# Low parts of dense weights computed on VectorE alone, and weighted expert scores made two experts ahead, in a two-block transformer kernel

## The chip, the cores and the metric

The kernel runs on one core of one Trainium2 chip, as one launch. The metric is the device time of that launch in microseconds (us). A chip core has TensorE (PE; its weight loads are listed apart as PEld), VectorE (DVE), ScalarE (ACT), GpSimd (POOL) and SyncE (SP), each with its own in-order queue, and DMA queues that move data between memory and the on-chip SBUF.

## The reference

Two blocks, in float32, on 256 tokens of width 1024.

The first block has two layers. Each layer is half a SwiGLU feed-forward (width 2816), a mixer, and half a second feed-forward:

```python
x = x + 0.5 * swiglu(rmsnorm(x, norm_g[i, 0]), ffn_w_up[i, 0], ffn_w_down[i, 0])
h = rmsnorm(x, norm_g[i, 1])
mix = pool_layer(...) if kind == 0 else diff_layer(...)   # DEPTH = 2: layer 0 pools, layer 1 attends
x = x + mix
x = x + 0.5 * swiglu(rmsnorm(x, norm_g[i, 2]), ffn_w_up[i, 1], ffn_w_down[i, 1])
```

The pooling layer takes windowed means, the differential layer subtracts two softmaxes per head, and both have four heads that attend to a memory of 256 tokens. The second block modulates its norms by six vectors made from `silu(c) @ w_ada`, runs a mixer of block attention and top-k attention (8 heads each, width 64), and ends in a layer of 16384 experts:

```python
q = (hc @ w_query).reshape(B, T_CHUNK, PEER_HEADS, 2, PEER_DKEY // 2)
s = jnp.einsum('bthpd,hpnd->bthpn', q, sub_keys)          # top 16 of 128 twice, then top 16 of 256 sums
g = jax.nn.softmax(g_s, axis=-1)
act = jax.nn.gelu(jnp.einsum('btd,bthkd->bthk', hc, u_emb[e_idx]), approximate=False)
return jnp.einsum('bthk,bthkd->btd', g * act, v_emb[e_idx])
```

## The kernel before

The kernel keeps all activations on chip and streams some 790 chunks of weights, each 128 x 1024 floats (512 KB), through four or five raw buffers. Every chunk is used in a three-product form. ScalarE rounds the raw chunk to a high part `whi` (line 144), a second engine computes the low part `wlo = raw - whi` (line 145), and TensorE adds three products: high by high, high by low, low by high (`mm3`, lines 184 to 186). The activations are split into high and low parts in the same way (`split_evac`, lines 194 and 195).

The order of work is the order in which the Python code emits instructions: the schedule is manual, and each engine runs its own instructions strictly in that order. The list `items` holds the chunks in order of use. `nextw` (line 153) hands the next chunk to TensorE's code, and before that emits the splits of the chunks up to `cfg["ahead"]` beyond it; `split_one` (line 130) emits one split: the load of a chunk further on, `whi` on ScalarE, `wlo` on VectorE or GpSimd. Which of the two is set in line 134 by `cfg["pool"]`: with 3, every third chunk goes to GpSimd; with 1, all of them; with 0, none. The feed-forward stages and projections run with 3, the attention stages (pooling layer's memory heads, differential attention, second block's attention, and the query projection of the experts) with 1 or 2, and the expert stages with 0.

In a feed-forward (`ffn`, line 499) each block of 512 up-columns makes a gate: VectorE multiplies the products by the row scale (line 524), ScalarE applies Silu, GpSimd multiplies by the row scale again (line 526), and VectorE multiplies by the second half of the products (line 536). Between the blocks VectorE also accumulates `silu(c) @ w_ada` (`ada_piece`, line 459, with the accumulation in line 469).

The attention stages are software pipelines (`pipeline`, line 50) of units: scores on TensorE, maximum and scale on VectorE (`nb`, line 865 in differential attention), exponential on ScalarE, normalization on VectorE (lines 878 and 880 there, 577 in memory heads, 1164 in the second block), transposition on TensorE. Weight projections are stepped between the units.

In the expert layer each block of 128 experts is called an expert here; there are NE = 128 of them. For each, a u chunk gives activations (`s_step`, line 1320: 24 matmuls of 256 columns, then Gelu on ScalarE in line 1331), and a v chunk gives outputs (12 matmuls of 512 columns for one expert). 78 of the u chunks are done before the first v chunk. After that the v chunks are mixed with the remaining 50 u chunks, one u after every two or three v. Before an expert's v products, `w_step` (line 1495) multiplies its activations by its routing weights: `wf` on VectorE (line 1497), `wh` on ScalarE (line 194), `wl` on VectorE (line 195). `w_step(n + 1)` is emitted at the start of expert n, right behind the split of a chunk two items on; the tiles `wf`, `wh`, `wl` have two buffers each. In this text the v stage is the stretch from the first v product (1624 us) to the end, and an item is one u or v chunk of it.

Of the kernel before, what the change touches and what calls it, by code (L numbers as in the profile page):

```python
# [9 lines left out]
F32 = mybir.dt.float32  # L10
F32R = mybir.dt.float32r
# [4 lines left out]
OP = mybir.AluOpType  # L16
# [3 lines left out]
P = 128  # L20
D = 1024
S = 256
# [7 lines left out]
NE = 128  # L30
# [29 lines left out]
def kernel(ctx: ExitStack, tc: tile.TileContext, A, LAY, stop=None):  # L60
    nc = tc.nc
    ctx.enter_context(tc.manual_schedule())
    V, ACT, G, PE = nc.vector, nc.scalar, nc.gpsimd, nc.tensor
# [39 lines left out]
    deferred = []  # L103
    cfg = {"raw": 5, "ahead": 4, "pool": 3, "phase": 0}
    CH = 1024
# [24 lines left out]
    def split_one():  # L130
        j = st["split"]
        load_to(j + cfg["raw"])
        _, nk, w, call = items[j][:4]
        eng = G if cfg["pool"] and (j + cfg["phase"]) % cfg["pool"] == 0 else V
        n = nk * w
        r = st["raw"].pop(j)
        if call is not None:
            call(r[:, :n].rearrange("p (k w) -> p k w", w=w))
        else:
            p_ = wpool2 if j < dense and st["nsplit"] % 2 else wpool  # L140
            st["nsplit"] += 1
            hi = p_.tile([P, CH], F32R, name="whi", tag="whi", bufs=4)
            lo = p_.tile([P, CH], F32R, name="wlo", tag="wlo", bufs=4)
            ACT.activation(hi[:, :n], r[:, :n], AF.Copy)  # L144
            eng.tensor_tensor(lo[:, :n], r[:, :n], hi[:, :n].bitcast(F32), op=OP.subtract)  # L145
            st["s"][j] = Split(hi[:, :n].rearrange("p (k w) -> p k w", w=w), lo[:, :n].rearrange("p (k w) -> p k w", w=w))
        st["split"] += 1
        load_to(j + 1 + cfg["raw"])
# [245 lines left out]
    def out_proj_k(segs, update, nxt, tail=2, ahead=None):  # L394


        p = [[pmm() for _ in range(2)] for _ in range(NT)]
        n = len(segs)

        def mm(t, h, gis, gots):  # L400
            for gi in gis:
                act, k0 = segs[gi]
                for c, k, _ in gots[gi][h]:
                    mm3(p[t][h], act[:, k0 + k, t * P:(t + 1) * P], c[:, k, :], gi == 0 and k == 0, gi == n - 1 and k == 1)

        gots = {}
        for gi in range(n - tail):
            gots[gi] = [fetch(1), fetch(1)]
            for t in range(NT):
                for h in range(2):  # L410
                    mm(t, h, [gi], gots)
                if t:
                    run_deferred()
                yield
        was = dict(cfg)
        cfg.update(ahead=8 - 2 * tail)
        if tail == 2 and nxt.deep:
            cfg["pool"] = 2
        for gi in range(n - tail, n):
            gots[gi] = [fetch(1), fetch(1)]  # L420
        cfg.update(was)
        for t in range(NT):
            for h in range(2):
                cut = n - 1 if nxt.deep and t and h else n
                mm(t, h, range(n - tail, cut), gots)
                if cut < n:
                    was = dict(cfg)
                    cfg.update(ahead=0, pool=1)
                    ahead.append(fetch(4))
                    nxt.realT(0)  # L430
                    mm(t, h, range(cut, n), gots)
                    if tail > 2:
                        split_more(1)
                update(t, h, p[t][h])
                nxt.pre(t, h)
                if not nxt.deep and (t or h):
                    nxt.T(*((0, 0), (0, 1), (1, 0))[2 * t + h - 1])
                if h:
                    nxt.stats(t)
                if cut < n:  # L440
                    if tail == 2:
                        cfg.update(pool=2, phase=1)
                    ahead.append(fetch(4))
                    cfg.update(was)
                yield
        if not nxt.deep:
            nxt.late = [lambda: nxt.T(1, 1)]
# [48 lines left out]
    def ffn(n, nxt, stk):  # L496
# [17 lines left out]
        for t, p in enumerate(proj_row(hT, 4, n.before)):  # L514
            r = n.rstd[:, t:t + 1]
            ACT.activation(s0[:, t], p[:, :256], AF.Silu, scale=r)
            V.scalar_tensor_tensor(g0[:, t], p[:, 256:], r, s0[:, t], op0=OP.mult, op1=OP.mult)
        rbb = bcast_rows(rb, n.rstd)
        for b in range(1, 11):
            s = fp.tile([P, 2, S], F32, name="silu", tag="silu", bufs=2)  # L520

            def evac(c0, m, p):
                if c0 == 0:
                    V.tensor_tensor(s, p, rbb, op=OP.mult)
                    ACT.activation(s, s, AF.Silu)
                    G.tensor_tensor(s, s, rbb, op=OP.mult)
                    flush()
# [161 lines left out]
    lo = [mem_T(0, 0), mem_T(0, 1)]  # L689
    cfg["pool"] = 0  # L690
    split_one()
# [3 lines left out]
    for f in lo:  # L695
        f()
    cfg.update(pool=3, phase=1, ahead=0)
    p = [pmm() for _ in range(NT)]
# [18 lines left out]
    for l in range(2):  # L717
# [8 lines left out]
        for i, _ in enumerate(proj_cols(mT, 4, 4, lambda c0, m, p, l=l: V.tensor_tensor(KT[l][:, c0:c0 + m, :], p, rbb, op=OP.mult))):  # L726
            if l == 0:
                n0.T(i // 2, i % 2)
    cfg["phase"] = 0
    sng = small([P, 1], "sng", bufs=1)  # L730
# [28 lines left out]
    with pool("pl") as sp:  # L759
# [45 lines left out]
        drain(u_part(0), proj_cols(hT, 4, 4, lambda c0, m, p: ACT.activation(qT[:, c0:c0 + m, :], p, AF.Copy)))  # L805
        cfg["pool"] = 1
        o = out_proj_k([(cat, k) for k in range(0, 12, 2)], plain_add, n2)
        fill = itertools.chain(u_part(1), mixed(), o)
        counts = [0, 1, 1, 0, 1, 1, 1, 2] + [1] * 6
        for n, _ in zip(counts, pipeline(units, [(1, 2), (3, 3), (None, 0), (0, 0), (2, 2)])):  # L810
            for _ in range(n):
                step(fill)
        cfg["pool"] = 3
        drain(fill)
# [15 lines left out]
    with pool("df") as sp:  # L830
# [119 lines left out]
        drain(qk(k[0]), qk(q[0]))  # L950
        cfg["pool"] = 1
        units = [make(t, h) for g in range(2) for t in range(NT) for h in (4 * g, 4 * g + 2)]
# [5 lines left out]
        for i, _ in enumerate(pipeline(units, [(5, 6), (1, 2), (4, 4), (None, 0), (6, 6), (0, 0), (3, 3), (2, 2)])):  # L958
            for _ in range(counts[i] if i < len(counts) else 1):
                step(fill)  # L960
        cfg["pool"] = 3
        drain(o)
# [106 lines left out]
    ACT.activation(iqT, iqp.rearrange("p (j t) -> p j t", j=2), AF.Copy)  # L1069
    cfg.update(pool=3, phase=1)  # L1070
    split_more(4)
    cfg.update(pool=3, phase=0)
    ACT.activation(av[:, 1, :512], mvp[1], AF.Copy)
# [127 lines left out]
    drain(*se)  # L1201
    cfg["pool"] = 1
    nhh = iter(("aq", "ak"))
# [84 lines left out]
    keep_rows(0, 1, q_rows(0, 1))  # L1288
    cfg["pool"] = 2
    split_more(4)  # L1290
# [3 lines left out]
    pop()  # L1294
    cfg["pool"] = 1
    late_scores = []
# [19 lines left out]
    dp = ctx.enter_context(pool("dq", side="right"))  # L1316
    cfg.update(raw=4, ahead=2, pool=0)
    act = {}
# [176 lines left out]
    def w_step(n):  # L1495
        wf = gpool.tile([P, S], F32, name="wf", tag="wf", bufs=2)
        V.tensor_tensor(wf.rearrange("p (g t) -> p g t", t=GT), act[n].rearrange("p (g t) -> p g t", t=GT), GW[n // GI][:, :, n % GI, :],  # L1497
                        op=OP.mult)
        W[n] = Split(gpool.tile([P, S], F32R, name="wh", tag="wh", bufs=2), gpool.tile([P, S], F32R, name="wl", tag="wl", bufs=2))
        split_evac(W[n][:, :], wf)  # L1500
# [12 lines left out]
    for i, (kind, arg) in enumerate(quanta):  # L1513
        if quanta[i + 1:i + 2] == [("v", (0, 0))]:
            w_step(0)
        if kind == "u":
            if half is None:
                half = s_step()
                next(half)
            else:  # L1520
                next(half)
                half = None
            continue
        n, t = arg[:2]
        if t == 0:
# [6 lines left out]
            vs[n], _, _ = nextw()  # L1532
            if n + 1 < NE:
                w_step(n + 1)
            if n % GI == 1 and n // GI + 1 < NE // GI and n // GI:
# [111 lines left out]
```

## Time and profile before

| | |
|---|---|
| median of three runs | 2187.47 us (2185.53 to 2187.62) |
| profiled execution | 2190.42 us |
| its span, first to last instruction | 2188.7 us |
| mean granted TensorE clock | 0.983 of full speed |
| PE busy | 2070.1 us (95%) |
| DVE busy | 1498.8 us (68%) |
| ACT busy | 986.0 us (45%) |
| POOL busy | 537.1 us (25%) |

The busy time of an engine is the union of its instructions' spans. Matmuls overlap in the records (one of 512 columns is listed with some 0.40 us, and the next starts some 0.23 us after it), so a share of busy time on PE is not a share of its peak. A row of waits names who ended the idle time of an engine and how long it was.

### The profile page before, as it was taken

To read this page: it belongs to the slowest core of one execution; us is meant where nothing else is said; L and a number is where in the kernel's file an instruction comes from. 1 tells how busy PE (TensorE), PEld (TensorE's weight loads), DVE (VectorE), ACT (ScalarE), POOL (GpSimd) and SP (SyncE) were. 2 spreads that over 40 slices of the span, in tenths; PEclk is the share of its full clock that TensorE was granted. 3 is DMA by queue.
4 is the path that set the end of the run, shared out by engine and by line. 5 is a ranking of instruction groups with operands and counts; after the bars stand their busy time and mean duration, and the time that the engine had idled before them with its cause. 6 is when DMAs were issued, how large, how long until landed. Compare 5 with 4: busy or idle time off the path is not lost. (4 is left out here: it accounts for less than half of the span.)

```text
span 2188.7 us, 34702 instructions
## 1 busy us (share of the span) xinstructions
PE 2070.1 (95%) x13678; PEld 1828.7 (84%) x13678; DVE 1498.8 (68%) x2202; ACT 986.0 (45%) x1508; POOL 537.1 (25%) x290
## 2 busy tenths in 40 slices
PE   8999989999999989999989999999999999999998
PEld 7998778998898788799878779999987777777775
DVE  6677556777677568665558879999955555555556
ACT  5444445444444445344444444455544444444443
POOL 3434334334343253543433532000000000000000
PEclk9999989999999999999999999999999999999999
DMA  7667534667567552355635344556775666675663
GB/s 253 210 233 239 199 117 166 231 229 247 186 223 235 197 193 89 116 188 198 220 106 174 97 147 135 183 173 227 245 246 187 204 190 202 202 221 185 210 192 125
DMA packets 142379, 416.94 MB, mean 190 GB/s; under 512 B 12468, under 2 KB 47428, under 8 KB 140040
## 3 DMA queue, kind: packets, MB, share of 16 engines
q1 hardware_dynamic: 102672, 372.04, 51.5%
q10 hardware_dynamic: 37976, 36.91, 5.3%
q0 software_dynamic: 1568, 5.77, 0.8%
q8 instruction: 107, 1.75, 0.3%
q14 instruction: 56, 0.46, 0.1%
HBM read 396.82 MB, written 17.86 MB: 189 GB/s over the span
## 5 line engine op out<-in xcount | busy, mean ns | idle before, releaser
L145 DVE TENSOR_TENSOR wlo<-raw,whi 128x1024 fp32r<-128x1024 f32 x478 | 704.3, 1488 | 382.7 <-ACT whi L144 377.6
L144 ACT ACTIVATE whi<-raw 128x1024 fp32r<-128x1024 f32 (+1 forms) x654 | 663.2, 1048 | 154.4 <-PE mm L186 68.3
L145 POOL TENSOR_TENSOR wlo<-raw,whi 128x1024 fp32r<-128x1024 f32 (+1 forms) x176 | 447.5, 2558 | 499.5 <-ACT whi L144 485.1
L184 PE MATMUL mm<-hT_hi,whi 128*128 128x256 f32 x1680 | 481.3, 286 | 0.0
L186 PE MATMUL mm<-hT_hi,wlo 128*128 128x256 f32 x1680 | 474.8, 283 | 1.7 <-DVE wlo L145 1.7
L185 PE MATMUL mm<-hT_lo,whi 128*128 128x256 f32 x1680 | 474.7, 283 | 0.0
L184 PEld LDWEIGHTS mm<-hT_hi,whi 128*128 128x128 f32 x1680 | 320.4, 191 | 6.4 <-issue 5.8
L186 PEld LDWEIGHTS mm<-hT_hi,wlo 128*128 128x128 f32 x1680 | 320.1, 191 | 2.3 <-DVE wlo L145 2.1
L185 PEld LDWEIGHTS mm<-hT_lo,whi 128*128 128x128 f32 x1680 | 320.2, 191 | 2.0 <-issue 1.9
L184 PE MATMUL sm<-hT_hi,whi 128*128 128x256 f32 (+1 forms) x1048 | 299.7, 286 | 2.8 <-ACT act L1331 1.5
L185 PE MATMUL sm<-hT_lo,whi 128*128 128x256 f32 (+1 forms) x1048 | 296.6, 283 | 1.6 <-DVE hT_lo L195 1.6
L186 PE MATMUL sm<-hT_hi,wlo 128*128 128x256 f32 (+1 forms) x1048 | 296.8, 283 | 0.5 <-DVE wlo L145 0.5
L184 PE MATMUL mm<-whi,wh 128*128 128x512 f32 x512 | 211.0, 412 | 37.1 <-ACT wh L194 36.3
L1552 POOL TENSOR_TENSOR fr<-fr,mhalf 128x1 f32<-128x1 f32 x2 | 1.5, 770 | 842.2 <-DVE fr L1551 842.2
L184 PEld LDWEIGHTS sm<-hT_hi,whi 128*128 128x128 f32 (+1 forms) x1048 | 199.0, 190 | 6.2 <-ACT act L1331 1.7
L186 PE MATMUL mm<-whi,wl 128*128 128x512 f32 x512 | 202.9, 396 | 0.0
L185 PEld LDWEIGHTS sm<-hT_lo,whi 128*128 128x128 f32 (+1 forms) x1048 | 199.1, 190 | 4.1 <-DVE hT_lo L195 2.1
L185 PE MATMUL mm<-wlo,wh 128*128 128x512 f32 x512 | 201.8, 394 | 0.0
L186 PEld LDWEIGHTS sm<-hT_hi,wlo 128*128 128x128 f32 (+1 forms) x1048 | 199.3, 190 | 1.0 <-DVE wlo L145 0.9
L184 PEld LDWEIGHTS mm<-whi,wh 128*128 128x128 f32 x512 | 96.3, 188 | 84.5 <-ACT wh L194 70.9
L194 ACT ACTIVATE wh<-wf 128x256 fp32r<-128x256 f32 x128 | 53.4, 417 | 217.0 <-DVE wf L1497 215.0
L1331 ACT ACTIVATE act<-sm 128x256 f32<-128x256 f32 x128 | 49.2, 384 | 222.0 <-PE sm L186 222.0
(306 smaller groups left out, 3123.8 us busy)
## 6 DMA issues: line engine op xcount, KB each, us to landing
raw<-in_ffn_up_dram SPq DMA_DIRECT2D x176, 512.0 KB, 4.5
raw<-in_peer_u_dram SPq DMA_DIRECT2D x128, 512.0 KB, 4.0
raw<-in_peer_v_dram SPq DMA_DIRECT2D x128, 512.0 KB, 3.5
raw<-in_ffn_dn_dram SPq DMA_DIRECT2D x88, 512.0 KB, 4.6
raw<-in_w_ada_dram SPq DMA_DIRECT2D x48, 512.0 KB, 4.4
gall<-stage ACTq DMA_DIRECT2D x16, 1024.0 KB, 6.6
G<-gall ACTq DMA_DIRECT2D x16, 1024.0 KB, 6.9
raw<-in_diff_w_in_dram SPq DMA_DIRECT2D x28, 512.0 KB, 4.6
```

The costliest lines, as they stand in the source:

```text
L144: ACT.activation(hi[:, :n], r[:, :n], AF.Copy)
L145: eng.tensor_tensor(lo[:, :n], r[:, :n], hi[:, :n].bitcast(F32), op=OP.subtract)
L184: PE.matmul(out, a[0], b[0], start=start, stop=False)
L185: PE.matmul(out, a[0], b[1], start=False, stop=False)
L186: PE.matmul(out, a[1], b[0], start=False, stop=stop)
L194: ACT.activation(hi, src, AF.Copy)
L1331: ACT.activation(act[n], p, AF.Gelu)
L1552: G.tensor_tensor(fr[:, t:t + 1], fr[:, t:t + 1], mhalf[:, :1], op=OP.pow)
```

## The change

Part one removes GpSimd from the dense stages' low parts: `split_one` always uses VectorE, and every place that set `cfg["pool"]` or `cfg["phase"]` loses that setting. GpSimd's second multiplication in the feed-forward (line 526) goes to VectorE too. Part two emits `w_step` for two experts before the first v product, and then `w_step(n + 2)` at the start of expert n, with three buffers for `wf`, `wh` and `wl`.

```diff
-    cfg = {"raw": 5, "ahead": 4, "pool": 3, "phase": 0}
+    cfg = {"raw": 5, "ahead": 4}
@@ split_one
-        eng = G if cfg["pool"] and (j + cfg["phase"]) % cfg["pool"] == 0 else V
...
-            eng.tensor_tensor(lo[:, :n], r[:, :n], hi[:, :n].bitcast(F32), op=OP.subtract)
+            V.tensor_tensor(lo[:, :n], r[:, :n], hi[:, :n].bitcast(F32), op=OP.subtract)
@@ out_proj_k (the other settings of "pool" and "phase" go in the same way)
-        if tail == 2 and nxt.deep:
-            cfg["pool"] = 2
...
-                    cfg.update(ahead=0, pool=1)
+                    cfg.update(ahead=0)
@@ ffn
-                    G.tensor_tensor(s, s, rbb, op=OP.mult)
+                    V.tensor_tensor(s, s, rbb, op=OP.mult)
@@ w_step
-        wf = gpool.tile([P, S], F32, name="wf", tag="wf", bufs=2)
+        wf = gpool.tile([P, S], F32, name="wf", tag="wf", bufs=3)
...
-        W[n] = Split(gpool.tile([P, S], F32R, name="wh", tag="wh", bufs=2), gpool.tile([P, S], F32R, name="wl", tag="wl", bufs=2))
+        W[n] = Split(gpool.tile([P, S], F32R, name="wh", tag="wh", bufs=3), gpool.tile([P, S], F32R, name="wl", tag="wl", bufs=3))
@@ loop over the quanta of the v stage
         if quanta[i + 1:i + 2] == [("v", (0, 0))]:
             w_step(0)
+            w_step(1)
...
-            if n + 1 < NE:
-                w_step(n + 1)
+            if n + 2 < NE:
+                w_step(n + 2)
```

How the rows of an engine's program move is shown at three places. In the lists that follow the numbers behind names are those of buffers.

VectorE at the beginning of the v stage, before: `act_13102`, `act_13135` and `act_13168` are the activations of experts 0, 1 and 2, and the `wlo` rows are the low parts of chunks two items ahead.

```order
L145 TENSOR_TENSOR wlo_17131<-raw_17002,whi_17130 128x1024
L1497 TENSOR_TENSOR wf_17150<-act_13102,G_16990 128x256
L195 TENSOR_TENSOR wl_17153<-wf_17150,wh_17152 128x256
L145 TENSOR_TENSOR wlo_17170<-raw_17035,whi_17169 128x1024
L1497 TENSOR_TENSOR wf_17175<-act_13135,G_16990 128x256
L195 TENSOR_TENSOR wl_17178<-wf_17175,wh_17177 128x256
L145 TENSOR_TENSOR wlo_17194<-raw_17068,whi_17193 128x1024
L1497 TENSOR_TENSOR wf_17199<-act_13168,G_16990 128x256
L195 TENSOR_TENSOR wl_17202<-wf_17199,wh_17201 128x256
```

The same place in the changed program:

```order
L144 TENSOR_TENSOR wlo_17131<-raw_17002,whi_17130 128x1024
L1481 TENSOR_TENSOR wf_17150<-act_13102,G_16990 128x256
L194 TENSOR_TENSOR wl_17153<-wf_17150,wh_17152 128x256
L1481 TENSOR_TENSOR wf_17156<-act_13135,G_16990 128x256
L194 TENSOR_TENSOR wl_17159<-wf_17156,wh_17158 128x256
L144 TENSOR_TENSOR wlo_17176<-raw_17035,whi_17175 128x1024
L1481 TENSOR_TENSOR wf_17181<-act_13168,G_16990 128x256
L194 TENSOR_TENSOR wl_17184<-wf_17181,wh_17183 128x256
```

The scores of expert 1 now stand before the first `wlo` of the stage instead of behind it, and those of expert 2 where those of expert 1 stood; the row order within one expert is the same.

VectorE in differential attention, before, at the normalization of the first unit (`e_7733` and `e_7736` are its two softmaxes, `e_7920` belongs to the third unit):

```order
L874 RECIPROCAL rc_7742<-sum_7741 128x2
L875 RECIPROCAL rc_7750<-sum_7749 128x2
L876 TENSOR_SCALAR rc_7750<-rc_7750,nlam_658 128x2
L878 TENSOR_SCALAR e_7736<-e_7736,rc_7750 128x128 x2
L880 SCALAR_TENSOR_TENSOR e_7733<-e_7733,rc_7742,e_7736 128x128 x2
L858 SCALAR_TENSOR_TENSOR e_7920<-nd_7334,sm_7914 128x256 x2
```

The same place in the changed program:

```order
L869 TENSOR_SCALAR e_7736<-e_7736,rc_7750 128x128 x2
L871 SCALAR_TENSOR_TENSOR e_7733<-e_7733,rc_7742,e_7736 128x128 x2
L144 TENSOR_TENSOR wlo_7866<-raw_7576,whi_7865 128x1024
L144 TENSOR_TENSOR wlo_7872<-raw_7682,whi_7871 128x1024
L144 TENSOR_TENSOR wlo_7878<-raw_7688,whi_7877 128x1024
L144 TENSOR_TENSOR wlo_7884<-raw_7694,whi_7883 128x1024
L849 SCALAR_TENSOR_TENSOR e_7920<-nd_7334,sm_7914 128x256 x2
```

Four low parts that stood in GpSimd's program now stand between the normalization of one unit and the first instruction of another.

VectorE at the entry of the expert routing, before (`qr` are rows of queries, `sc` scores whose 16 largest are searched by MAX, MAX_INDEX and MATCH_REPLACE):

```order
L1269 COPY qr_12515<-mm_12452 128x512
L1269 COPY qr_12542<-mm_12517 128x512
L145 TENSOR_TENSOR wlo_12585<-raw_12432,whi_12584 128x1024
L145 TENSOR_TENSOR wlo_12597<-raw_12444,whi_12596 128x1024
L1241 MAX v160_12506<-sc_12607 128x8 x4
```

The same place in the changed program:

```order
L1255 COPY qr_12542<-mm_12517 128x512
L144 TENSOR_TENSOR wlo_12579<-raw_12309,whi_12578 128x1024
L144 TENSOR_TENSOR wlo_12585<-raw_12432,whi_12584 128x1024
L144 TENSOR_TENSOR wlo_12591<-raw_12438,whi_12590 128x1024
L144 TENSOR_TENSOR wlo_12597<-raw_12444,whi_12596 128x1024
L1227 MAX v160_12506<-sc_12607 128x8 x4
```

The two low parts of this group that GpSimd had are now in VectorE's row too; the groups of four and of two that follow in this stretch, wholly GpSimd's before, join it in the same way.

## Rows read from the trace of the kernel before

**Rows 1.** The page, part 1: busy us, share and instructions of each engine.

```profile
PE 2070.1 (95%) x13678; PEld 1828.7 (84%) x13678; DVE 1498.8 (68%) x2202; ACT 986.0 (45%) x1508; POOL 537.1 (25%) x290
```

**Rows 2.** Stages, busy us (count): PE, PEld, DVE, ACT, POOL; clock, DMA share, GB/s.

```profile
335.00:795.00 460.00, 449.81 (x2989) 407.10 (x2988) 315.74 (x287) 197.31 (x243) 169.48 (x82) 1.00 0.65 218
795.00:910.00 115.00, 101.05 (x649) 88.31 (x649) 91.84 (x185) 56.68 (x151) 64.52 (x30) 0.93 0.34 113
...
1300.00:1345.00 45.00, 44.72 (x350) 42.77 (x349) 39.79 (x227) 22.86 (x31) 21.89 (x10) 1.00 0.33 106
...
1624.00:2180.00 556.00, 518.75 (x2712) 416.46 (x2712) 316.42 (x437) 241.63 (x357) 0.00 (x0) 1.00 0.61 192
```

**Rows 3.** Waits, 1623 to 2163 us: total us, times, longest.

```profile
PE mm L184 <- ACT wh L194: 36.3, 51, 0.7
```

**Rows 4.** Timeline, 1852 to 1863 us: start, duration, what [idle before <-releaser].

```profile
1853.74 0.28 PE L184 MATMUL sm<-hT_hi,whi 128*128 128x256 f32 x1
...
1856.56 0.40 PE L184 MATMUL mm<-whi,wh 128*128 128x512 f32 x1
...
1856.76 0.38 ACT L1331 ACTIVATE act<-sm 128x256 f32<-128x256 f32 x1 [1.94 <-PE sm L186]
...
1857.04 1.05 ACT L144 ACTIVATE whi<-raw 128x1024 fp32r<-128x1024 f32 x1
...
1858.12 1.23 DVE L145 TENSOR_TENSOR wlo<-raw,whi 128x1024 fp32r<-128x1024 f32 x1 [2.05 <-ACT whi L144]
...
1859.14 0.40 PE L186 MATMUL mm<-whi,wl 128*128 128x512 f32 x1
1859.26 0.42 DVE L1497 TENSOR_TENSOR wf<-act,G 128x256 f32<-128x256 f32 x1
...
1859.78 0.42 ACT L194 ACTIVATE wh<-wf 128x256 fp32r<-128x256 f32 x1 [1.69 <-DVE wf L1497]
...
1860.24 0.50 PE L184 MATMUL mm<-whi,wh 128*128 128x512 f32 x1 [0.71 <-ACT wh L194]
...
1862.32 0.42 DVE L1497 TENSOR_TENSOR wf<-act,G 128x256 f32<-128x256 f32 x1
```

**Rows 5.** Groups of instructions by line and shape: count | busy us, mean ns | idle before.

```profile
L145 DVE TENSOR_TENSOR wlo<-raw,whi 128x1024 fp32r<-128x1024 f32 x478 | 704.3, 1488 | 382.7 <-ACT whi L144 377.6 <-issue 4.9
...
L145 POOL TENSOR_TENSOR wlo<-raw,whi 128x1024 fp32r<-128x1024 f32 x172 | 440.3, 2575 | 498.6 <-ACT whi L144 484.2 <-PE mm L186 5.3 <-issue 4.6
...
L536 DVE TENSOR_TENSOR gate<-mm,silu 128x512 f32<-128x512 f32 x40 | 27.7, 692 | 70.1 <-POOL silu L526 49.2 <-PE mm L186 20.9
```

**Rows 6.** Line L469: duration ns min/median/max.

```profile
L469 DVE SCALAR_TENSOR_TENSOR acc<-raw,cols,acc x84: 737/752/2906, 83.7 to 715.5; 128x512 f32<-128x512 f32 x84
```

**Rows 7.** Groups of instructions, 1623 to 2163 us.

```profile
L145 DVE TENSOR_TENSOR wlo<-raw,whi 128x1024 fp32r<-128x1024 f32 x173 | 212.1, 1226 | 167.6 <-ACT whi L144 167.6
```

**Rows 8.** Timeline, 811 to 819 us, in differential attention.

```profile
811.31 9.34 POOL L145 TENSOR_TENSOR wlo<-raw,whi 128x1024 fp32r<-128x1024 f32 x4 [5.69 <-ACT whi L144]
811.36 4.72 DVE L878 TENSOR_SCALAR e<-e,rc 128x128 f32<-128x128 f32 x2
...
816.01 4.79 DVE L880 SCALAR_TENSOR_TENSOR e<-e,rc 128x128 f32<-128x128 f32 x2
...
818.50 0.33 PE L243 MATMUL tr<-ident,e 128*128 128x128 f32 x1 [4.38 <-DVE e L880]
```

**Rows 9.** Waits of PE, 0 to 1345 us.

```profile
PE tr L243 <- DVE e L880: 8.8, 5, 4.4
...
PE tr L1257 <- ACT pqU L1301: 0.2, 1, 0.2
```

**Rows 10.** Line 145 alone by stage: stretch, DVE busy (x), POOL busy (x).

```profile
795.00:910.00 115.00, 0.00 (x0) 60.50 (x26) 0.93 0.34 113
...
1115.00:1345.00 230.00, 25.46 (x16) 88.30 (x37) 0.94 0.38 126
```

**Rows 11.** Timeline of VectorE, 1262 to 1345 us.

```profile
1304.67 5.99 DVE L145 TENSOR_TENSOR wlo<-raw,whi 128x1024 fp32r<-128x1024 f32 x2 [8.33 <-ACT whi L144]
```

More of the change, by code (lines that the diff above doesn't have):

```diff
@@ L440, in out_proj_k @@
                 if cut < n:
-                    if tail == 2:
-                        cfg.update(pool=2, phase=1)
                     ahead.append(fetch(4))
@@ L689 @@
     lo = [mem_T(0, 0), mem_T(0, 1)]
-    cfg["pool"] = 0
     split_one()
@@ L696 @@
         f()
-    cfg.update(pool=3, phase=1, ahead=0)
+    cfg.update(ahead=0)
     p = [pmm() for _ in range(NT)]
@@ L728 @@
                 n0.T(i // 2, i % 2)
-    cfg["phase"] = 0
     sng = small([P, 1], "sng", bufs=1)
@@ L805 @@
         drain(u_part(0), proj_cols(hT, 4, 4, lambda c0, m, p: ACT.activation(qT[:, c0:c0 + m, :], p, AF.Copy)))
-        cfg["pool"] = 1
         o = out_proj_k([(cat, k) for k in range(0, 12, 2)], plain_add, n2)
@@ L812 @@
                 step(fill)
-        cfg["pool"] = 3
         drain(fill)
@@ L950 @@
         drain(qk(k[0]), qk(q[0]))
-        cfg["pool"] = 1
         units = [make(t, h) for g in range(2) for t in range(NT) for h in (4 * g, 4 * g + 2)]
@@ L960 @@
                 step(fill)
-        cfg["pool"] = 3
         drain(o)
@@ L1069 @@
     ACT.activation(iqT, iqp.rearrange("p (j t) -> p j t", j=2), AF.Copy)
-    cfg.update(pool=3, phase=1)
     split_more(4)
-    cfg.update(pool=3, phase=0)
     ACT.activation(av[:, 1, :512], mvp[1], AF.Copy)
@@ L1201 @@
     drain(*se)
-    cfg["pool"] = 1
     nhh = iter(("aq", "ak"))
@@ L1288 @@
     keep_rows(0, 1, q_rows(0, 1))
-    cfg["pool"] = 2
     split_more(4)
@@ L1294 @@
     pop()
-    cfg["pool"] = 1
     late_scores = []
@@ L1316 @@
     dp = ctx.enter_context(pool("dq", side="right"))
-    cfg.update(raw=4, ahead=2, pool=0)
+    cfg.update(raw=4, ahead=2)
     act = {}
```

## The prediction

> **What bounds the kernel now.** I read the page's totals first, then the stages, then in the stage that the second part of the change touches the waits and the timeline, and last the durations of VectorE's instructions beside GpSimd's. The totals [rows 1] show PE busy for 95% of the span, DVE for 68%, POOL for 25%: an engine order in which work moved from POOL to DVE should cost nothing on average, so what counts is where PE waits. The stages [rows 2] show two kinds. In the feed-forward stretch from 335 to 795 us PE is busy for 449.8 of 460 us; there nothing that DVE does is worth much. In differential attention (795 to 910) PE is busy for 101 of 115 us, DVE for 92 and POOL for 65, so that DVE is the one that is waited for. In the v stage (1624 to 2180) PE is busy for 518.8 of 556 us, and POOL does nothing.
>
> In the v stage all idle time of PE has one releaser: ACT's `wh`, 51 times, 36.3 us [rows 3]. The timeline shows how it comes about [rows 4]. A u item ends on PE at 1856.56. ACT's Gelu of it runs at 1856.76, behind it in ACT's queue `whi` of a chunk at 1857.04, behind that on DVE its `wlo` at 1858.12, behind that in DVE's queue `wf` of the next expert at 1859.26, then `wh` on ACT at 1859.78. PE has finished the expert before by then and starts on the new one at 1860.24. From the end of the u item to `wh` ready is 3.7 us, and one expert lasts 2.8: the scores are made one expert ahead, and the chain is longer than one expert. Between two v items without a u the same ring (`wf`, `wh`, `whi`, `wlo`, `wf`) takes 1862.32 - 1859.26 = 3.06 us, again more than 2.8.
>
> **The v stage, step by step.** An item's time on PE without a wait is read from the starts of matmuls, since their listed ends overlap: a u item is 1856.56 - 1853.74 = 2.82 us [rows 4]; in the v item behind it 11 spacings take 1859.14 - 1856.56 = 2.58 us, so 12 take 2.81. The stage has 128 v and 50 u items: 178 x 2.82 = 502 us against some 555 that it takes. So 53 us are lost. The smaller 36.3 us of the waits is the same loss less what the modelled ends of matmuls cover; a stall that is listed with 0.71 us opens 1.10 us between two starts (1859.14 and 1860.24) where 0.23 is the rule, so it costs 0.87.
>
> With the scores two experts ahead, `wh` of expert n + 2 is ready 3.7 us behind the end of a u item and is wanted two or more items behind it, 5.6 us or later. The waits go if the ring keeps up. I lay it out for u, v, v, from the u's end at 0: Gelu 0.2, `whi` 0.48, `wlo` 1.56, `wf` 2.70, `wh` 3.22; one ring later, 3.06 us, `wf` 5.76 and `wh` 6.28, which lasts 0.42; then `whi` of the next u's split, 6.7 to 7.75. The next Gelu can't start before 8.4 (three items). ACT is free 0.65 us before that; with three v between two u it is free at 10.8 against 11.2. So the ring is shorter than PE's work over a whole period although it is longer over one v item, and the second buffered expert lets it make that good. What is late next: the chunks' own low parts, which are still two items ahead (`wlo` of the first v's split is ready at 2.8, wanted at 5.6), and the DMAs. The stage moves 192 GB/s at a share of 0.61; in 502 us the same bytes are 213 GB/s, below the 218 of the feed-forward stretch [rows 2]. The third buffer means that `wh` and `wl` of n + 2 overwrite those of n - 1, whose products ended when expert n began: no new wait. `w_step(1)` ahead of the stage adds 0.9 us on DVE and 0.4 on ACT beside u items. I take 53 us; the bounds are 36 (the waits alone) and 56 (PE's plain sum with all else gone too).
>
> [...] By PE's busy time the stage would have 37 us to give, by the weight loads (416.5 of 556) 139; by the spacing of starts it is 53, between the two, and the spacing is what I use.
>
> **The dense stages.** What moves: 176 low parts, 172 of them full chunks [rows 5], and 40 products of the feed-forward. On DVE without POOL beside it a full `wlo` takes 1.226 us, as in the v stage where POOL is idle [rows 7]; the 40 products take about what line 536 does, 0.69 [rows 5]. That adds 176 x 1.23 + 40 x 0.69 = 244 us to DVE. What it gives back: over the whole run a `wlo` on DVE takes 1.488 [rows 5], so 478 x (1.488 - 1.226) = 125 us go; the accumulations of `w_ada` take 0.75 in the median and up to 2.9 [rows 6], which is where the mean of the stretched ones lies. In differential attention the stretching is plain: while four `wlo` run on POOL from 811.31 for 9.34 us, two scalings of 128 x 128 take 4.72 and two combinations 4.79 on DVE, each ending with one of POOL's, and PE waits 4.38 us for the second [rows 8]. So DVE gets at most 244 - 125 = 119 us more work net over 1345 us, and isn't full on average. The products at line 526 are hidden: DVE's line 536 waited 49.2 us for them on POOL [rows 5], and PE is full there.
>
> On the path stands what PE waits for: 21 rows of releasers on DVE, ACT or POOL up to 1345 us, from 8.8 us down to 0.2, 57 us together [rows 9], of which the first and the last are shown. Those for results behind stretched DVE instructions (`e` in the three attentions 8.8 + 6.8 + 5.0, low parts of `hT` 6.5 + 3.2, `acc` 8.0, a scale 2.2) are 40 us. I take 60% of it as given back, 24 us, since a burst of four `wlo` in DVE's row still delays what stands behind it by 4.9 us where two stretched ones took 6 to 7.
>
> Against it stand the places where POOL had all low parts and DVE was needed. In differential attention and from 1115 to 1345 us those are 26 + 37 = 63 [rows 10]. Most bursts fall where DVE has already delivered, as in the second place of the order shown. Two don't. At the routing entry (1300 to 1345) DVE is busy for 39.8 of 45 us [rows 2] and without a pause from 1304.67 on; 8 low parts more are 9.8 us, two that took 5.99 [rows 11] shrink to 2.5, and an earlier start gives 1 back: 5 us late into a stretch where PE takes u items as DVE makes them, so 5 us. And in the second block's attention one burst stands right before a normalization; 4 us. So the dense stages give 24 - 9 = 15 us. The bounds: 57 (every such wait gone) and -77 (all 63 low parts laid bare at 1.23); I hold 40 given to 25 lost as the likely part.
>
> [...]
>
> **Sum.** 2190.4 (the profiled execution) - 53 - 15 = 2122. That execution lies 2.95 us above the median of the runs, so 2119 for the median.
>
> **Rivals.** First, slower than before: DVE's row becomes the bound in the attentions. Place: the bursts of four in differential attention, the second block's attention and the routing entry. Each `wlo` waits for `whi`, so a burst holds what is queued behind it on DVE (maxima, scales, normalizations), for which ACT's exponentials and PE's transposes wait. 63 low parts at 1.23 are 77 us, 24 more than the v stage gives: 2190.4 - 2.95 - 53 + 77 = 2211. It decides from 43 exposed low parts on. For it: DVE is busy for 92 of 115 us in differential attention. Against it: much of that 92 is stretched (in rows 8 four small instructions take 9.5 us, until POOL is done).
>
> Second, the ring stays the bound of the v stage: a third buffer does nothing for a ring that is 3.06 us long, and only the waits behind a u item go. Then 128 x (3.06 - 2.81) = 32 us of the loss stay, 21 come: 2190.4 - 2.95 - 21 - 15 = 2151. For it: the ring's length in rows 4. Against it: the 0.4 to 0.65 us left in each period.
>
> Third, DMA: chunks land late at the higher rate. If an item takes 2.95 us instead of 2.82, 23 of the 53 us go: 2142. For it: the loads of G (1 MB) fall into the same queues; against it, the 218 GB/s above.
>
> Fourth, the change doesn't do what it says: `wf` stays behind the same `wlo` in DVE's row, or a buffer wait pins it, and PE waits as before; then 2190.4 - 2.95 - 15 = 2172.
>
> **How the numbers follow.** The forecast has 0.70, the first rival 0.09, the second 0.10, the third 0.05, the fourth 0.06. The forecast's own range is 2094 to 2159 (40 given to 25 lost in the dense stages). With the second and third rival inside and a little below for the v stage's 56, I give 2090 to 2160. About 0.2% (4 us) is what a measurement here tells from no change: faster by more 0.88 (all of the forecast, most of the rivals but the first), within it 0.03, slower 0.09.
>
> **What would show it.** In the profile after: no wait of PE on `wh` in the v stage, and that stage some 502 us long (step right), or still waits of 0.3 us between v items (second rival), or waits on `whi` released by DMA (third). `wlo` on DVE at a mean near 1.23 us, no POOL rows but the small ones, and the scalings of rows 8 under 1 us. PE's waits in the attentions at about half. The forecast is wrong if PE's waits on `e`, `hT_lo` or `wlo` before 1345 us grow beyond their 57, or if u items between 1345 and 1624 us wait for `wlo` by more than 5.

## The result and the profile after

The changed kernel takes 2107.07 us in the median of four runs (2104.82 to 2109.91), the kernel before beside it 2187.55 (2185.53 to 2192.68): the ratio is 0.963, with a 95% interval of 0.961 to 0.965. The forecast was 2119, 12 us too high. The profiled execution has a span of 2105.6 us and a mean granted clock of 0.986.

Part 1 of the page after answers to [rows 1].

```profile
PE 2037.7 (97%) x13678; PEld 1834.5 (87%) x13678; DVE 1481.0 (70%) x2418; ACT 985.6 (47%) x1508; POOL 39.0 (2%) x74
```

DVE has 216 instructions more and is busy for 18 us less: by these two numbers POOL had stretched DVE's work by some 262 us, more than the 244 us that DVE took over (both are estimates). The prediction counted 125 us of it, in the low parts alone; the accumulations of `w_ada`, for example, fell from 1.07 to 0.75 us in the mean as well.

To see where the time went I cut both runs at the same events: the first `u` write of the pooling heads, the first `k` of differential attention, its last `cat_hi`, the first `aq` of the second block, the first routing row `qr`, the first v product, the last matmul. The columns are those of [rows 2]. First before, then after:

```profile
0.00:265.75 265.75, 252.96 (x1671) 231.50 (x1672) 180.00 (x176) 122.35 (x158) 102.58 (x80) 0.99 0.67 227
265.75:782.19 516.44, 498.10 (x3220) 447.61 (x3218) 348.23 (x338) 223.91 (x290) 188.08 (x90) 0.98 0.60 204
782.19:908.80 126.61, 112.66 (x753) 100.18 (x753) 98.02 (x189) 60.37 (x155) 68.79 (x31) 0.93 0.38 127
908.80:1164.02 255.22, 245.82 (x1571) 219.04 (x1569) 145.75 (x143) 115.68 (x164) 97.16 (x54) 0.98 0.53 174
1164.02:1295.05 131.03, 121.52 (x768) 100.61 (x768) 109.44 (x231) 58.58 (x128) 57.04 (x25) 0.94 0.37 124
1295.05:1624.45 329.40, 320.29 (x2990) 313.33 (x2991) 296.36 (x686) 162.50 (x256) 21.89 (x10) 0.99 0.61 202
1624.45:2179.70 555.25, 518.73 (x2712) 416.46 (x2712) 316.10 (x437) 241.06 (x356) 0.00 (x0) 1.00 0.61 193
```

```profile
0.00:257.64 257.64, 249.48 (x1671) 228.37 (x1672) 175.43 (x216) 122.27 (x159) 14.31 (x41) 1.00 0.67 234
257.64:749.99 492.35, 490.17 (x3210) 443.26 (x3208) 333.53 (x415) 223.59 (x290) 6.46 (x10) 1.00 0.62 214
749.99:876.53 126.54, 112.57 (x763) 101.22 (x762) 90.29 (x213) 60.22 (x155) 4.07 (x4) 0.93 0.36 121
876.53:1128.14 251.61, 244.40 (x1570) 218.42 (x1568) 151.29 (x187) 115.87 (x164) 9.62 (x13) 0.99 0.54 180
1128.14:1261.65 133.51, 120.56 (x768) 100.88 (x768) 107.85 (x254) 58.51 (x128) 2.60 (x3) 0.95 0.37 121
1261.65:1597.66 336.01, 322.87 (x2990) 316.14 (x2990) 301.65 (x694) 162.12 (x255) 0.43 (x1) 0.98 0.61 198
1597.66:2096.70 499.04, 497.59 (x2712) 426.17 (x2712) 316.09 (x437) 241.47 (x356) 0.00 (x0) 1.00 0.68 214
```

Stage by stage the difference is -8.1, -24.1, -0.1, -3.6, +2.5, +6.6 and -56.2 us: -26.8 up to the first v product and -56.2 behind it. More than half of the -24.1 stands in the part of that stage with the feed-forwards, from the last `cat_lo` of the pooling layer to the first `k`, first before, then after: 13.4 us, and PE's 10.2 us of idle time are gone altogether.

```profile
329.79:782.19 452.40, 442.21 (x2902) 398.49 (x2901) 311.57 (x285) 198.20 (x244) 168.42 (x81) 1.00 0.64 215
```

```profile
310.96:749.99 439.03, 439.03 (x2892) 397.18 (x2891) 302.35 (x355) 197.88 (x244) 6.46 (x10) 1.00 0.64 221
```

The idle time of PE (length less busy) and the clock column tell the same stages apart. Idle time up to the first v product goes from 73.1 to 57.6 us. PE's busy time for the same 10,966 matmuls falls too, from 1551.3 to 1540.1. Nearly all of that second fall is the clock's: cut into stretches of 5 us, (1 - granted clock) x length adds up to 35.8 us before the first v product in the run before, and 25.6 after. What a low stretch looks like, in the run before, its PE waits from 675 to 688 us and then two stretches:

```profile
PE sm L477 <- DVE acc L469: 3.2, 1, 3.2
```

```profile
680.00:685.00 5.00, 1.81 (x14) 1.34 (x13) 4.96 (x4) 0.83 (x1) 2.35 (x1) 1.00 0.87 274
685.00:690.00 5.00, 5.00 (x26) 4.41 (x25) 1.48 (x3) 2.31 (x4) 1.27 (x1) 0.66 0.66 231
```

PE stands still for 3.2 us of the first stretch, for an `acc` that POOL had stretched (two accumulations took 3.62 us from 680.97 on, beside a low part that POOL made from 680.90 to 683.25; after, one takes 0.75); in the second it is busy throughout at a mean granted clock of 0.66, with 26 matmuls where full stretches nearby have 44 or 45. The 3.2 us wait was followed by a loss of another 0.34 x 5 = 1.7 us.

In the v stage, the waits after (1597 to 2097 us) answer to [rows 3], and the timeline from 1811 to 1823 us to [rows 4].

```profile
PE mm L183 <- ACT wh L193: 2.0, 2, 1.4
```

```profile
1811.79 0.42 ACT L193 ACTIVATE wh<-wf 128x256 fp32r<-128x256 f32 x1 [1.71 <-DVE wf L1481]
...
1813.97 0.28 PE L183 MATMUL sm<-hT_hi,whi 128*128 128x256 f32 x1
...
1816.78 0.40 PE L183 MATMUL mm<-whi,wh 128*128 128x512 f32 x1
...
1816.98 0.38 ACT L1315 ACTIVATE act<-sm 128x256 f32<-128x256 f32 x1 [0.74 <-PE sm L185]
...
1819.49 0.42 DVE L1481 TENSOR_TENSOR wf<-act,G 128x256 f32<-128x256 f32 x1
1820.00 0.42 ACT L193 ACTIVATE wh<-wf 128x256 fp32r<-128x256 f32 x1 [1.69 <-DVE wf L1481]
...
1822.39 0.28 PE L183 MATMUL sm<-hT_hi,whi 128*128 128x256 f32 x1
1822.55 0.42 DVE L1481 TENSOR_TENSOR wf<-act,G 128x256 f32<-128x256 f32 x1
```

The chain from the end of the u item is as long as before: `wh` 3.2 us behind it, the next `wf` one ring (3.06 us) after the first. But the v item at 1816.78 starts without waiting for it: its `wh` is the one of 1811.79 or older. From u to u (1813.97 to 1822.39) three items take 8.42 us, 2.81 each. The Gelu's idle time of 0.74 us is the slack of the ring.

VectorE's low parts, up to the first v product and in the v stage, answer to [rows 5] and [rows 7]; the scalings of the first units of differential attention to [rows 8].

```profile
L144 DVE TENSOR_TENSOR wlo<-raw,whi 128x1024 fp32r<-128x1024 f32 (+1 forms) x479 | 565.2, 1221 | 201.0 <-ACT whi L143 200.7
...
L144 DVE TENSOR_TENSOR wlo<-raw,whi 128x1024 fp32r<-128x1024 f32 x175 | 214.5, 1226 | 113.4 <-ACT whi L143 113.4
```

```profile
780.30 0.49 DVE L869 TENSOR_SCALAR e<-e,rc 128x128 f32<-128x128 f32 x2
780.71 0.61 DVE L871 SCALAR_TENSOR_TENSOR e<-e,rc 128x128 f32<-128x128 f32 x2
```

None of these is stretched any more: 1.22 us a low part in the mean in the first place and 1.23 in the second, and 0.49 and 0.61 us where [rows 8] have 4.72 and 4.79. Yet the waits of PE up to 1337 us, which answer to [rows 9], have not halved in the differential and the second block's attention; others stand there:

```profile
PE tr L242 <- DVE cat_lo L200: 5.1, 2, 4.3
PE tr L242 <- DVE rc L866: 4.6, 1, 4.6
...
PE sm L185 <- DVE wlo L144: 3.9, 1, 3.9
```

### The profile page after: what moved, and what is told of

Same layout as the page of the kernel before. It is cut to its first block, busy times and chain, and to the rows that moved or that the text cites. A ratio compares the mean times of both kernels' runs of the same rounds, so it can differ in the third digit from the quotient of the medians.

```text
span 2105.6 us, 34581 instructions
## 1 busy us (share of the span) xinstructions
PE 2037.7 (97%) x13678; PEld 1834.5 (87%) x13678; DVE 1481.0 (70%) x2418; ACT 985.6 (47%) x1508; POOL 39.0 (2%) x74
## 3 DMA queue, kind: packets, MB, share of 16 engines
q0 software_dynamic: 1568, 5.77, 0.9%
## 5 line engine op out<-in xcount | busy, mean ns | idle before, releaser
L144 DVE TENSOR_TENSOR wlo<-raw,whi 128x1024 fp32r<-128x1024 f32 (+1 forms) x654 | 779.8, 1222 | 314.4 <-ACT whi L143 314.1
L183 PE MATMUL mm<-whi,wh 128*128 128x512 f32 x512 | 204.1, 399 | 2.0 <-ACT wh L193 2.0
L185 PE MATMUL mm<-whi,gT_lo 128*128 128x512 f32 x352 | 139.9, 397 | 0.0
L183 PE MATMUL mm<-whi,gT_hi 128*128 128x512 f32 x352 | 139.4, 396 | 0.0
L184 PE MATMUL mm<-wlo,gT_hi 128*128 128x512 f32 x352 | 138.8, 394 | 0.0
```

The source lines that it names most:

```text
L144: V.tensor_tensor(lo[:, :n], r[:, :n], hi[:, :n].bitcast(F32), op=OP.subtract)
L183: PE.matmul(out, a[0], b[0], start=start, stop=False)
L184: PE.matmul(out, a[0], b[1], start=False, stop=False)
L185: PE.matmul(out, a[1], b[0], start=False, stop=stop)
```

## The experiments

Theory: (a) the v stage gains by depth, since scores made two experts ahead are ready before PE wants them; (b) the dense stages gain because DVE is no longer held up by POOL, and lose a part where bursts of low parts stand in DVE's row. The rivals stand in the expectations. Each total is a median, its ratio to the kernel before in brackets; "first v" is the start of the first v product in the profiled run, "stretch" the time from there to the last matmul.

**One part alone.** The v part on the kernel before:

```
+ bufs=3 for wf, wh, wl;  w_step(0), w_step(1) ahead of the stage;  w_step(n + 2) in item n
```

> The kernel before with the second part of the change alone (scores two experts ahead, three buffers); GpSimd keeps its low parts in the dense stages. Theory (the two parts are independent; the v stage gains by depth, the dense stages by an undisturbed VectorE): the first v product stays at 1624 us, the stretch from it to the last matmul falls from 555 to 499, total 2187 - 56 = 2131. Rival (the v stage's gain needs the first part, because VectorE enters it with another backlog): total above 2140.

Measured: 2134.68 us (0.976, 0.974 to 0.978); first v 1624.8, stretch 499.0. The other part alone, the changed kernel with `bufs=2`, `w_step(n + 1)`:

> The changed kernel with scores one expert ahead in two buffers again, so the first part of the change alone. Theory: first v product at 1598 us, as in the changed kernel, v stretch 555 as before; total 2187 - 27 = 2160. The forecast on record gave this part 15, so 2172; a rival that the dense stages gain nothing by themselves (their 27 being a shift that the v stage made possible) gives 2187.

Measured: 2162.04 us (0.988, 0.986 to 0.990); first v 1599.0, stretch 556.0. The parts add up: 53 and 25 us of the 80.

**Buffers without depth.** The changed kernel with

```
- w_step(0); w_step(1)        + w_step(0)
- w_step(n + 2)               + w_step(n + 1)
```

> The changed kernel with three buffers but scores one expert ahead. Theory (depth decides: at one ahead the chain weighting, high part, low part, product is still as long as an item pair; the third buffer only frees a place that nobody waits for): v stretch 555, total as with the first part alone, 2160. Rival (the wait was for the buffer, not for the order of issue): v stretch 499, total 2107.

Measured: 2161.13 us (0.988, 0.986 to 0.990); stretch 552.8. The first product of a chunk, in the groups of the run with the v part alone and of this one:

```profile
L184 PE MATMUL mm<-whi,wh 128*128 128x512 f32 x512 | 204.0, 398 | 2.0 <-ACT wh L194 2.0
```

```profile
L183 PE MATMUL mm<-whi,wh 128*128 128x512 f32 x512 | 210.8, 412 | 35.4 <-ACT wh L193 35.0
```

35 us of waits on `wh` stay with three buffers and go with depth. The fourth rival of the prediction is out, and so is the second. One step further, four buffers and `w_step(n + 3)`:

> The changed kernel with scores three experts ahead in four buffers. Theory: at two ahead no product waits for the scores any more but one of 1.4 us near the end and 0.6 at the start, so the total stays within 2 us of 2107. Rival (depth still limits by the Gelu's slack): total 2103 or less.

Measured: 2107.76 us (0.965, 0.962 to 0.967), stretch 498.0: no more to be had there.

**Contention alone** (POOL at work beside DVE, and slowing it). The changed kernel, with a copy that nobody reads wherever POOL made a low part before:

```
  V.tensor_tensor(lo, r, hi, op=subtract)
+ if eng is G:                       # the choice of the kernel before
+     for a in range(0, n, 256):
+         G.tensor_tensor(scr, r[a:a + 256], hi[a:a + 256], op=subtract)
```

> The changed kernel, in which GpSimd makes a second copy of those low parts that it made before the change, in pieces of 128x256 into a scratch tile that nobody reads; the used low parts all stay with VectorE. Theory (the dense gain comes from VectorE no longer being held up by GpSimd): the mean 128x1024 low part on VectorE goes from 1.22 back to about 1.45 us or more and the dense stages lose at least the 27 us that they had gained: first v product at 1625 or later, total 2135 to 2170. Rival (the gain came from VectorE's low parts being ready sooner than GpSimd's, 1.2 against 2.4 us and in order, and what GpSimd does beside them costs nothing): total 2107 within 5.

Measured: 2210.61 us (1.011, 1.009 to 1.012), first v 1700.5, stretch 499.0. The low parts before 1590 us on DVE, and the copies on POOL:

```profile
L150 POOL TENSOR_TENSOR scr<-raw,whi 128x256 fp32r<-128x256 f32 (+1 forms) x700 | 805.1, 1150 | 480.5 <-ACT whi L144 273.1 <-issue 157.7 <-POOL scr L150 1.6
...
L145 DVE TENSOR_TENSOR wlo<-raw,whi 128x1024 fp32r<-128x1024 f32 (+1 forms) x454 | 655.8, 1486 | 174.1 <-ACT whi L144 173.3
```

The direction is the theory's, the size was beyond its range: in quarters the copies take 805 us of POOL, not 447, and they also hold the loaded weights, so that ACT's `whi` waited longer for DMA (44.9 and 33.9 us at its two largest groups of loads, 19.0 and 13.4 in the changed kernel). So the run was made again with half of the copies, on data that frees nothing else:

```
-         G.tensor_tensor(scr, r[a:a + 256], hi[a:a + 256], op=subtract)     # a = 0, 256, 512, 768
+         G.tensor_tensor(scr, hi[a:a + 256], hi[a:a + 256], op=subtract)    # a = 0, 256
```

> The changed kernel with GpSimd writing nothing that is read: at each low part that it made before the change it subtracts two quarters (128x256) of the high part from themselves into a scratch tile, so it doesn't touch the loaded weight and can't hold its buffer; its time is then about 175 x 2 x 1.15 = 400 us in place of 805 in the run with whole copies. Theory (contention between the two engines): the dense loss falls about as GpSimd's time does, 103 x 400 / 805 = 51; first v product 1625 to 1655, total 2132 to 2165, and VectorE's mean 128x1024 low part in the dense stages is above 1.3 us. Rival (whole copies cost because they held the loaded weights and delayed transfers): total 2107 to 2115.

Measured: 2139.20 us (0.979, 0.977 to 0.981), first v 1629.8.

```profile
L145 DVE TENSOR_TENSOR wlo<-raw,whi 128x1024 fp32r<-128x1024 f32 (+1 forms) x468 | 626.7, 1380 | 170.5 <-ACT whi L144 169.4
...
L151 POOL TENSOR_TENSOR scr<-whi 128x256 fp32r<-128x256 f32 x352 | 397.8, 1130 | 753.7 <-ACT whi L144 734.8
```

398 us of useless work on POOL, for which other instructions waited only 2.7 us in all (ACT, until a high part had been read), cost 32 us. Contention is shown, and it is enough for the whole 27 us. The rival that POOL's low parts simply came late is small by the trace of the kernel before: PE waited 0.9 us for them, its weight loads 1.7. The cost lies within the theory's range, but below its proportion (51); what the weights' buffers cost in the run before it is not told apart from that.

The same for the 40 products behind the Silu, back on POOL in the changed kernel:

```
- V.tensor_tensor(s, s, rbb, op=mult)        + G.tensor_tensor(s, s, rbb, op=mult)
```

> The changed kernel with the 40 products behind the feed-forward's Silu on GpSimd again. Theory (contention is paid by GpSimd's busy time): 40 x 1.3 = 53 us beside VectorE stretch it by about 262 x 53 / 537 = 26 us, against 29 us that VectorE gets rid of; total within 4 us of 2107. Rival (the dense gain lies mostly in these products, which stand between the Silu and the down product): the two feed-forwards lose most of their 14 us, total 2117 or more.

Measured: 2104.12 us (0.962, 0.960 to 0.963): within 4 us, as the theory has it. This piece of the change is worth nothing that can be measured.

**Where the low parts cost in DVE's row.** POOL again has those at the routing entry alone, 10 of them (8 before the change, when one group was shared between the two engines):

```
+ cfg["pool"] = 1        # low parts on POOL from here to the v stage's pool
  split_more(4)
```

> The changed kernel, in which GpSimd makes the low parts of the weights that are split between the start of the routing's rows and the v stage's pool (the table's 4 and the chunks after them), as before the change; everything ahead stays with VectorE. Theory (at the routing entry the low parts stand in VectorE's row ahead of its maxima and copies; the maxima and their indices aren't held up by GpSimd): the stretch from the first rows to the first v product falls from 336 to 329, total 2101. Rival (the 6.6 us came from the place where the stage before left off): 2107.

Measured: 2105.13 us (0.963, 0.961 to 0.965), no difference from 2107 that can be told. In the trace the part between `qr` and the first routing one-hot `oh` falls from 179.7 to 175.3 us, as the theory has it: the 3.9 us on `wlo` is gone. Behind it 2.4 us are lost again at one place far behind the last of these low parts, ACT's issue of two loads of G. After, and in this run:

```profile
1581.27 3.27 ACTq L1470 DMA_DIRECT2D G<-gall  x2
```

```profile
1577.80 4.79 ACTq L1472 DMA_DIRECT2D G<-gall  x2
```

The Gelu is queued behind it, and PE waits 4.1 us for it here, 1.7 after. POOL having all from the second block's attention on (34 low parts, some more than it had there before, since it takes the shared groups whole):

```
  drain(*se)
+ cfg["pool"] = 1
```

> As the run with GpSimd at the routing entry, but GpSimd has the low parts from the second block's attention on (aq's second half, its output products and the routing), as before the change. Theory: the attention gives back the 2.5 us that it had lost and the routing entry its 6.6, total 2098; rival (contention in that attention costs as much as the places in VectorE's row): 2101 or more, no better than the run with the routing entry alone.

Measured: 2099.41 us (0.961, 0.959 to 0.963), from 2098.22 to 2102.47 where the changed kernel had 2104.82 to 2109.91: no time of one lies among those of the other, though the intervals of the two ratios (0.961 to 0.965 for the changed kernel) overlap. The attention takes 128.4 us in place of 133.5, less than the 131.0 of before, and the stretch up to the first v product 334.1 in place of 336.0. So the theory's total was met, but not its parts: the attention gave 5.1 us, not 2.5, and the routing stretch 1.9, not 6.6. The change had gone too far in that attention. The rival is out there: POOL's time costs less than DVE's row.

Differential attention, which the change left at 126.5 us, on top of that run, with every second low part on POOL, and with all:

```
  drain(qk(k[0]), qk(q[0]))
+ cfg["pool"] = 2        # and 1 in the other run
```

> The run with GpSimd from the second block's attention on, and in the differential attention every second low part on GpSimd too (before the change it had all of them there, after it none). The change left this stage at 126.6 us (before) and 126.5 (after). Theory (two costs cancel there, what GpSimd stretches and what stands in VectorE's row in bursts of four): half and half shortens the burst and halves the stretch, so the stage falls to about 121 to 124, total 2094 to 2097. Rival (neither costs anything there; the stage is bounded by something that the change doesn't touch): stage 126.5, total 2099.

> As the run with every second low part, but GpSimd has all of them in the differential attention, as before the change. Theory and its rival both expect the stage at about 126.6 and the total at 2099; if it comes to 2094 or less, VectorE's row alone held the stage back; if to 2104 or more, contention alone.

Measured: 2108.66 us (0.963, 0.962 to 0.965), stage 136.5, for the half; 2099.84 (0.960, 0.958 to 0.961), stage 128.0, for all. The second is near what was expected (126.6 and 2099). The first is what neither theory had: shared, the same work is slowest, so that a bound which the low parts don't touch is out too. A burst of four in this run, and in the changed kernel:

```profile
823.18 5.63 POOL L145 TENSOR_TENSOR wlo<-raw,whi 128x1024 fp32r<-128x1024 f32 x2
...
823.84 6.06 DVE L145 TENSOR_TENSOR wlo<-raw,whi 128x1024 fp32r<-128x1024 f32 x2 [1.72 <-ACT whi L143]
...
831.49 0.66 PE L243 MATMUL tr<-ident,e 128*128 128x128 f32 x2 [6.87 <-DVE cat_lo L201]
```

```profile
817.71 4.63 DVE L144 TENSOR_TENSOR wlo<-raw,whi 128x1024 fp32r<-128x1024 f32 x4 [0.78 <-ACT whi L143]
...
823.94 0.66 PE L242 MATMUL tr<-ident,e 128*128 128x128 f32 x2 [4.26 <-DVE cat_lo L200]
```

From 823.18 to 829.90 the two engines make two low parts each in 6.7 us; alone each would take 2 x 2.4 us (POOL, by its low parts in the run that this one is built on) and 2 x 1.2 (DVE), 7.3 us in a row. Side by side 4.9 would do; the 6.7 measured are closer to one after the other, and what holds the two engines up the traces don't show. DVE by itself makes four in 4.63, and `cat_lo`, for which PE waits, is queued behind. The theory's error, by this burst, was to halve the stretch with the count: beside a DVE that had a burst of its own, POOL's two low parts fell on DVE work, whose two took 6.06 us in place of 2.4.

**The clock.** The run with POOL from the second block on, with one wait of 4.28 us filled:

```
+ f = pmm()
+ for _ in range(28):
+     PE.matmul(f[:, :256], hT.hi[:, 0, :P], hT.hi[:, 1, :])      # nobody reads f
  p = ptr()                                                       # s2 of the unit h = 6, t = 0
```

> The run with GpSimd from the second block's attention on, with 28 matmuls of 128x256 that nobody reads (28 x 0.118 = 3.3 us) put into one wait of TensorE in the differential attention, the one of 4.28 us in which it stood idle until the low part of cat was written (818.97 to 823.25 us of that run). There the matmuls from 824.2 to 827.4 us start every 0.21 us where 0.118 is the rule, and the granted clock from 820 to 830 us is below 1.00. Theory (the clock fell because TensorE stood idle, and each wait of some us is paid a second time by it): the wait falls to about 1 us, the matmuls behind it keep 0.118, the granted clock of that place 1.00, and cat's stage is 1.7 us shorter; total 2097.7, within what repeats differ by. Rival (the clock falls there whatever TensorE does): the matmuls behind the place are as slow as before and the stage as long, 125.7 us, or longer.

Measured: 2095.62 us (0.959, 0.957 to 0.962), not to be told from 2099.41; what counts is the place. PE's timeline and two stretches, first without and then with the filler:

```profile
823.25 0.41 PE L243 MATMUL tr<-ident,e 128*128 128x128 f32 x2 [4.28 <-DVE cat_lo L201]
...
824.22 0.41 PE L184 MATMUL mm<-hT_hi,whi 128*128 128x256 f32 x1
824.43 0.41 PE L185 MATMUL mm<-hT_lo,whi 128*128 128x256 f32 x1
```

```profile
820.00:825.00 5.00, 1.75 (x12) 1.78 (x13) 4.96 (x9) 0.32 (x1) 0.00 (x0) 0.92 0.81 293
825.00:830.00 5.00, 5.00 (x35) 5.00 (x34) 3.11 (x13) 2.35 (x9) 0.00 (x0) 0.74 0.26 102
```

```profile
819.17 3.59 PE L880 MATMUL mm<-hT_hi 128*128 128x256 f32 x28
823.68 0.41 PE L243 MATMUL tr<-ident,e 128*128 128x128 f32 x2 [0.92 <-DVE cat_lo L201]
...
824.28 0.28 PE L184 MATMUL mm<-hT_hi,whi 128*128 128x256 f32 x1
824.40 0.28 PE L185 MATMUL mm<-hT_lo,whi 128*128 128x256 f32 x1
```

```profile
820.00:825.00 5.00, 4.08 (x36) 3.90 (x35) 4.96 (x9) 0.75 (x2) 0.00 (x0) 1.00 0.89 290
825.00:830.00 5.00, 5.00 (x44) 4.94 (x43) 3.54 (x13) 2.58 (x10) 0.00 (x0) 1.00 0.29 116
```

`cat_lo` comes no sooner, but the matmuls behind it start 0.12 us apart in place of 0.21, the granted clock is 1.00 where it had been 0.92 and 0.74 (1.7 us), and the stage is 1.3 us shorter (124.4 against 125.7). In all seven traces that have this wait unfilled, of 4.26 to 4.28 us (the changed kernel and six runs on it, the one shown among them), the clock of these two stretches was 0.63 to 0.92 and 0.58 to 0.77 every time. At this place the clock fell because PE had stood still.

## Why the prediction was right, step by step

- **V stage, 53 us: right, measured 56.** No wait on `wh` but two, 2.0 us together, neither in the middle; 499.0 us where 502 were worked out, 178 items at 2.80. 56 was the upper bound. The ring came out as laid out: from the end of the u item at 1816.78, Gelu 0.2, `wf` 2.71 and 5.77, `wh` 3.22, and a slack at the Gelu of 0.74 where 0.4 to 0.65 was worked out. DMA carried 214 GB/s (213 forecast). Depth was the cause (2134.68 with it on the kernel before, 2161.13 with buffers alone).
- **Durations: right.** 1.22 us a low part, scalings of 0.49 and 0.61 us, where under 1 was forecast.
- **Dense stages, 24 given less 9 lost: the direction was right, the term mis-sized, 26.8 in place of 15.** Its sum of waits came out: PE's idle time fell by 4.6, 16.2 and 2.2 us in three stages (23.0 in all, 24 forecast) and rose by 3.4 and 4.0 in the second block's attention and from the routing on (7.5, 9 forecast), 15.5 in all. That is partly luck, since the places were others. Half of the 40 us that the 24 were taken from (20.6) are waits for `e` in three attentions, and of the stages that hold them only the pooling layer's heads (3.1 of the 20.6) became shorter. Of the feed-forward stretch from 335 to 795 us the prediction said that nothing that DVE does is worth much there; cut at the same events, it gave 13.4 us, 10.2 of waits and 1.7 of clock among them. The step also left out that a wait can be paid for a second time, by the granted clock: 35.8 us of clock became 25.6, and 15.5 + 10.2 = 25.7 of the 26.8. The filled wait shows this mechanism at one place of some 1.7 us. That all of the 10.2 is of this kind is not shown. In twelve runs (the two kernels and the ten experiments but the last and the one three ahead) the start of the first v product less PE's idle time and less the clock's loss is 1509 to 1516 us, while that start itself moves between 1588 and 1700, so nothing else of size is left; but waits and clock don't go in step in every stage: in the second block's attention PE's idle time rose by 3.4 us and the clock's loss fell from 8.4 to 6.8.
- **"PE's waits in the attentions at about half": wrong in two of three.** In the pooling layer's heads PE's idle time fell from 8.2 to 2.2 us. In the second block's attention it rose from 9.5 to 13.0. In differential attention they were 14.0 us idle before and after, only behind other results (`cat_lo`, `rc`, `xscale` in place of `e`). The step counted [rows 8] as given back at 60% there; it was 0, since four low parts stand in DVE's row where four stood on POOL. The gain came from the stages where DVE's row is not full: 16.2 us of idle time between 266 and 782 us of the old run, nearly all of the 18.3 that were there.
- **The losses: right.** 9 forecast, 9.1 measured: the stretch from the routing on became 6.6 us longer (5 forecast), the second block's attention 2.5 (4 forecast). With the low parts on POOL again the attention gave 5.1; the routing entry gave 4.4 in one run, but 1.7 in the run that had the attention's on POOL too.
- **Rivals.** A DVE row that becomes the bound (2211) shows at its three places, in the second block's attention and the routing as a loss of 9.1 us, in differential attention as a gain that did not come; the 77 us of 63 bare low parts were far off. The ring, DMA and a change without effect are out by the v stretch of 499.0 and 552.8. The loads of G, which the third rival put into the chunks' queues, are issued by ACT in the trace (all 16), those of the chunks by SP.

The forecast of 2119 was thus 12 us too high: 3 in the v stage, 12 in the dense term, and 3 the other way in the offset between profiled execution and median.

## What to carry to other kernels

Where PE waits for a chain that is longer than one item but shorter than a period, it takes depth, not buffers: here the v stretch was 499 us with depth, 553 with the buffers alone and 555 before. Where a helper slows the engine beside it, as POOL did DVE here (a low part up to the first v product took 1.64 us in the mean before, 1.22 after), taking its work over pays in stages where that engine's row has room, and costs where results are queued behind a burst: decide by stage. Don't split one burst between the two: here that was the slowest of three ways (136.5 us against 125.7 and 128.0). Where the granted clock is seen to fall behind PE's waits, price them with it: here 10.2 us less of clock loss came with 15.5 us less of waits.

## What the runs showed of the hardware that was not expected

- The clock fell behind a single wait. Behind 3.2 us of standing still, in the kernel before, the next stretch of 5 us had a mean granted clock of 0.66; behind 4.26 us, in the changed kernel, matmuls came every 0.21 us in place of 0.12 from 824.6 to 829.1 us, and every 0.12 again from 829.3 on, while PE was at work throughout. In the run with 28 matmuls in that wait the granted clock of the two stretches there was 1.00. It also fell among shorter waits: in the pooling layer's heads before, with no wait above 2.0 us, it cost 6.8 us.
- Two low parts on POOL and two on DVE took 6.7 us together, four on DVE 4.63.
- An issue of two loads by ACT held its queue for 3.27 us in one run and 4.79 in another (2.96 in the kernel before), and the Gelus behind it. The traces don't show what it waited for.
